# Dense attention of a hybrid encoder layer: value products three pairs behind the scores instead of two, and the dilated queries' gain multiplied on VectorE instead of GpSimd

## The chip, the cores and the metric

The kernel runs on one core of one Trainium2 chip. The metric is the device time of one execution in microseconds (us). The time before is the median of three runs, 1239.23 us (lowest 1236.90, highest 1239.25).

Short names of the engines, as the profile has them: PE is TensorE (matmul), PEld its weight loads, DVE is VectorE, ACT is ScalarE, POOL is GpSimd, SP is the engine that issues most DMAs.

## What is computed

One encoder layer on 1024 positions of 1024 features, all in float32. After a normalisation and one projection the heads go two ways. Group A (8 query heads, 2 key/value heads, 64 wide) is dense attention. Group B (8 heads) is a mixture of three dilated windows. Both outputs are normalised and projected, and a gated feed-forward block with a width-3 convolution follows. The parts that matter here:

```
hn = rms_norm(x, norm1_g);  proj = hn @ w_in          # -> qA kA vA qB kB vB
qa = apply_axial_rope(rms_norm(qa, qa_norm_g));  ka = the same with ka_norm_g
out_a = softmax(qa @ ka.T / 8) @ va                   # dense, all 1024 keys, per head
out_b = dilated_mixture_attention(rms_norm(qb, qb_norm_g), rms_norm(kb, kb_norm_g), vb)
x = x + concat(rms_norm(out_a), rms_norm(out_b)) @ w_out
x = x + conv_ffn(rms_norm(x, norm2_g))
```

The last step of the norm of qb, the multiplication by `qb_norm_g` (with the key's gain and the scale folded in), is what the second half of the change moves.

## The kernel before

The program runs in stages on one core: the input projection (0 to 212 us of the span), dense attention (212 to 387), dilated attention (387 to about 560), and then the output projection and the feed-forward block. All tensors of a stage lie at fixed offsets in two large arrays, `bigf` (float32) and `bigr` (float32 as TensorE multiplies it), and PSUM is one array `ps` of 8 banks of 512 columns. Float32 products are made of two or three products of a rounded high part and a rounded low part.

**Dense attention** is `a_main_bounded`, called for 16 groups g. A group is 128 queries (g // 2) of one key/value head (g % 2) with its four query heads, so a matmul has 512 columns. Its 1024 keys are taken in four pairs j of two tiles of 128 keys. For one pair:

- PE makes the scores: 4 matmuls (L763, L764) into two banks of PSUM. Two pairs of banks alternate, so the scores of pair n+2 wait until the exponential of pair n has read its banks.
- ACT takes the exponential of 1024 columns (L769) from PSUM into a float32 buffer `F_PB`.
- The high part is a copy of it (L773 on ACT; for j = 1 it is L771 on DVE) into `R_PHB`; the low part is a subtraction on DVE (L774) into `R_PLB`. There are two buffers `F_PB` and three of each of the others, used in turn.
- PE makes the value products `pv(j)`: 6 matmuls (L747), two for the high part of either tile and one for the low part. They accumulate over the group in one bank.

`pv(j)` is written two pairs behind the scores: `pv(0)` and `pv(1)` in steps 2 and 3 of their own group, `pv(2)`, `pv(3)` in steps 0 and 1 of the next. After `pv(3)` DVE copies the sums out (L757), PE turns them (L752), and DVE divides by the denominator (L792, L793). That turn (`o_turn`) is written into step 3 of the next group.

**Other work is spread over these groups.** The queries of the next group are split (L661 on ACT, L662 on DVE), turned on PE (L190) and copied (L678 on ACT). A table `spread`, by group and tile, holds what the projection left over: three additions (L444), the rotary step of two pieces of qa (POOL L528, L302; DVE L535, L538), two pieces of w_out (ACT L1060, DVE L1065), and the norm of the four pieces of qb: a square on ACT (L558), its mean on DVE (L510, L511), a root, `norm_at` on DVE (a 1-column copy L554, a 16-column copy L574, a multiplication of 1024 columns L575), and `gain` on POOL (L541, 1024 columns). The last two stand together in `spread[10 + i, 0]`. From group 14 on, the first head of the dilated stage is prepared: POOL splits its queries (L662 on POOL, after ACT's L661), PE turns them, POOL issues a DMA that copies keys (L868).

**What sets the order.** The instructions of an engine run in the order in which a scheduler in the framework puts them when the program is built; within an engine nothing overtakes. Code that is written later can so be put earlier. To hold a step back, the kernel writes one column of the step's destination from something that is ready late (`hold`, L1294; the copies L554, L1307, L1309). `now`, in `a_main_bounded`, is that something: the output of an earlier group, or the next group's queries.

The code for larger gains (`bounded` false) is in the program as well, behind a branch; it isn't run here.

Of the kernel before, what the change touches and what calls it, by code (L numbers as in the profile page):

```python
# [15 lines left out]
OP = mybir.AluOpType  # L16
# [28 lines left out]
R_XT = 0  # L45
# [37 lines left out]
R_VA = R_XT + 9248  # L83
R_PHB = (R_PH, R_PH + 1024, R_XT + 1024)
R_PLB = (R_PL, R_PL + 1024, R_XT + 3072)
F_PB = (O_F, O_F + 2560)
F_OT = O_F + 1024
# [47 lines left out]
def tile_encoder_layer(ctx, tc, x, w_in, gains, outg, norm1_g, norm2_g, w_out, w_up, conv_w, conv_b,  # L135
# [14 lines left out]
    def emit(bounded):  # L150
# [326 lines left out]
        def done(c, t0, u, late=None):  # L477
# [61 lines left out]

            def gain():  # L540
                gp.tensor_tensor(q3, q3, fp(O_GB, [0, 4], [0, 4], [1, 64]), op=OP.mult)  # L541

# [33 lines left out]

            return square_at, mean_at, root_at, refine_at, norm_at, gain

# [152 lines left out]

        pairs = [1]

        def a_main_bounded(g, prep, tail, late, plan, late_plan):
# [24 lines left out]
            for j in range(4):  # L759
# [6 lines left out]
                pairs[0] += 1  # L766
                p, ph, pl = F_PB[n % 2], R_PHB[n % 3], R_PLB[n % 3]
                slots[j] = ph, pl
# [6 lines left out]
                for kt in (2 * j, 2 * j + 1):  # L775
                    take(prep, plan[kt])
                    take(late, late_plan[kt])
                    now = f(qab((g - 1) // 2) + 256 * ((g - 1) % 2), 1) if 0 < kt < 7 else \
                        rf(R_Q2A + 512 * ((g + (kt == 7)) % 2), 1)
                    for step in spread.pop((g, kt), []):  # L780
                        step(now)
                step = tail.pop(0) if tail else None
                if step:
                    step()
                if j > 1:
                    pv(j - 2)

            return [lambda: pv(2), last, None, o_turn]

# [501 lines left out]
        if bounded:  # L1291
# [4 lines left out]
            def run(ts, o=None):  # L1296
                def at(now):
                    if o is not None:
                        hold(o, now)
                    for t in ts:  # L1300
# [6 lines left out]
                      (2, 2): [lambda now: vec.tensor_copy(f(F_KN[0], 1), now)] + run(first[:5]),  # L1307
                      (3, 0): run(first[5:6], F_KN[0]), (3, 3): run(first[6:], F_OS),
                      (3, 6): [lambda now: vec.tensor_copy(f(F_KN[0], 1), now)] + run(turns[:5]),  # L1309
                      (4, 5): run(turns[5:6], F_KN[0]), (5, 0): run(turns[6:], F_OS)}  # L1310
        for i, d in enumerate(deferred[2:]):
            square_at, mean_at, root_at, refine_at, norm_at, gain = done(*d, i)
            spread[5 + i, 2] = [square_at]
            spread[5 + i, 7] = [mean_at]
            if i == 3:
                spread[9, 3] = [root_at]
                spread[9, 7] = [refine_at]
            spread[10 + i, 0] = [norm_at, lambda now, gain=gain: gain()]

# [553 lines left out]
```

## Time and profile before

| | us |
|---|---|
| median of three runs | 1239.23 |
| the profiled execution's own time | 1239.64 |
| its span, first to last instruction | 1237.7 |
| outside the span | 1.9 |
| dense attention, 212 to 387 us: length | 175.0 |
| PE busy in it | 167.1 |
| DVE busy in it | 144.9 |
| ACT busy in it | 140.5 |
| POOL busy in it | 34.2 |

The profile is one execution, taken by the hardware profiler. Busy time of PE is the time covered by at least one matmul. Matmuls overlap: one of 512 columns is listed with about 0.39 us, and the next starts 0.23 us after it. So a waiting PE shows as idle a little later than it really had nothing to start, and slower matmuls show as a busy PE. The table of the stage by windows also has the granted clock of TensorE (PEclk, 1.00 is full).

In rows of the timeline the columns are start, duration, engine, line, operation, tiles and shapes, the number of instructions merged, and in brackets the idle time before with what ended it.

### The profile page before, as it was taken

To read this page: it belongs to the slowest core of one execution; us is meant where nothing else is said; L and a number is where in the kernel's file an instruction comes from. 1 tells how busy PE (TensorE), PEld (TensorE's weight loads), DVE (VectorE), ACT (ScalarE), POOL (GpSimd) and SP (SyncE) were. 2 spreads that over 40 slices of the span, in tenths; PEclk is the share of its full clock that TensorE was granted. 3 is DMA by queue.
4 is the path that set the end of the run, shared out by engine and by line. 5 is a ranking of instruction groups with operands and counts; after the bars stand their busy time and mean duration, and the time that the engine had idled before them with its cause. 6 is when DMAs were issued, how large, how long until landed. Compare 5 with 4: busy or idle time off the path is not lost.

```text
span 1237.7 us, 17828 instructions
## 1 busy us (share of the span) xinstructions
PE 1198.8 (97%) x6615; PEld 1010.7 (82%) x6615; DVE 1008.1 (81%) x1315; ACT 670.8 (54%) x968; POOL 403.6 (33%) x302
## 2 busy tenths in 40 slices
PE   7999999999899989999999999999999999999998
PEld 7999998666568988888788888888888888888886
DVE  4988687789888989656999999999999997876663
ACT  7856555789788766634554434453444544443341
POOL 1610114120223330011356666576755743000000
PEclk9999999999999999999999999999999999999999
DMA  7036403010004544422222332223232247977872
GB/s 277 25 101 159 112 4 75 1 33 17 1 9 108 134 112 133 156 81 77 94 90 89 111 106 106 88 98 114 94 110 94 88 160 253 353 235 245 280 234 92
DMA packets 120925, 147.00 MB, mean 119 GB/s; under 512 B 51009, under 2 KB 79489, under 8 KB 120321
## 3 DMA queue, kind: packets, MB, share of 16 engines
q1 hardware_dynamic: 119329, 140.05, 35.4%
q0 software_dynamic: 1504, 5.77, 2.3%
q8 instruction: 53, 0.87, 0.3%
q14 instruction: 39, 0.32, 0.1%
HBM read 107.25 MB, written 33.82 MB: 114 GB/s over the span
## 4 chain that ended last, share of the span: by engine, by line
PE 56%; DVE 17%; issue 5%; ACT 3%; DMA 1%; POOL 1%; SPq 0%; DVEq 0%; ACTq 0%; POOLq 0%
DVE bigf L1570 7%; PE ps L1537 6%; PE ps L1539 6%; PE ps L1538 6%; PE ps L1670 6%; PE ps L1669 6%; PE ps L1671 6%; PE ps L747 5%; DVE bigf L1541 2%; PE ps L1111 2%; PE ps L1112 2%; PE ps L1110 2%; DVE bigr L1521 2%; DVE bigr L774 2%; PE ps L763 2%
## 5 line engine op out<-in xcount | busy, mean ns | idle before, releaser
L1537 PE MATMUL ps<-bigr 128*128 128x512 f32 x616 | 241.1, 392 | 6.3 <-DVE bigf L1541 5.7
L1539 PE MATMUL ps<-bigr 128*128 128x512 f32 x616 | 239.7, 389 | 0.0
L1538 PE MATMUL ps<-bigr 128*128 128x512 f32 x616 | 239.7, 389 | 0.0
L1570 DVE SCALAR_TENSOR_TENSOR bigf<-bigf 128x768 f32<-128x768 f32 (+1 forms) x176 | 178.6, 1073 | 26.4 <-ACT bigf L1568 26.3
L1520 ACT ACTIVATE bigr<-bigf 128x512 fp32r<-128x512 f32 x154 | 93.2, 625 | 139.6 <-POOL bigf L1512 70.2
L1649 ACT ACTIVATE bigr<-bigf 128x1024 fp32r<-128x1024 f32 (+1 forms) x99 | 83.6, 867 | 116.0 <-PE ps L1671 74.2
L1537 PEld LDWEIGHTS ps<-bigr 128*128 128x128 f32 x616 | 115.6, 188 | 34.9 <-DVE bigf L1541 9.1
L1539 PEld LDWEIGHTS ps<-bigr 128*128 128x128 f32 x616 | 115.6, 188 | 24.2
L1538 PEld LDWEIGHTS ps<-bigr 128*128 128x128 f32 x616 | 115.7, 188 | 23.6
L432 PE MATMUL ps<-bigr 128*128 128x256 f32 x448 | 128.1, 286 | 1.1 <-ACT bigf L308 1.1
L433 PE MATMUL ps<-bigr 128*128 128x256 f32 x448 | 127.6, 285 | 0.4 <-DVE bigr L416 0.4
L1521 DVE TENSOR_TENSOR bigr<-bigf,bigr 128x512 fp32r<-128x512 f32 x112 | 125.1, 1134 | 3.2 <-ACT bigr L1520 2.8
L434 PE MATMUL ps<-bigr 128*128 128x256 f32 x448 | 127.4, 284 | 0.0
L1670 PE MATMUL ps<-bigr 128*128 128x512 f32 x308 | 119.8, 389 | 0.0
L1669 PE MATMUL ps<-bigr 128*128 128x512 f32 x308 | 119.8, 389 | 0.0
L1671 PE MATMUL ps<-bigr 128*128 128x512 f32 x308 | 119.8, 389 | 0.0
L1650 DVE TENSOR_TENSOR bigr<-bigf,bigr 128x1024 fp32r<-128x1024 f32 (+1 forms) x99 | 96.7, 995 | 26.4 <-ACT bigr L1649 24.3
L747 PE MATMUL ps<-bigr 128*66 128x512 f32 x384 | 103.6, 404 | 5.0 <-DVE bigr L774 4.8
L774 DVE TENSOR_TENSOR bigr<-bigf,bigr 128x1024 fp32r<-128x1024 f32 x64 | 84.6, 1333 | 16.1 <-ACT bigr L773 15.5
L432 PEld LDWEIGHTS ps<-bigr 128*128 128x128 f32 x448 | 86.5, 193 | 1.8 <-ACT bigf L308 1.5
L433 PEld LDWEIGHTS ps<-bigr 128*128 128x128 f32 x448 | 86.6, 193 | 0.6 <-DVE bigr L416 0.6
L434 PEld LDWEIGHTS ps<-bigr 128*128 128x128 f32 x448 | 86.6, 193 | 0.0
(230 smaller groups left out, 2513.2 us busy)
## 6 DMA issues: line engine op xcount, KB each, us to landing
bigf<-w_down SPq DMA_DIRECT2D x99, 256.0 KB, 4.3
bigf<-w_up SPq DMA_DIRECT2D x44, 512.0 KB, 3.6
bigf<-gscr SPq DMA_DIRECT2D x77, 256.0 KB, 4.2
gscr<-bigf SPq DMA_DIRECT2D x31, 512.0 KB, 2.6
bigf<-w_in SPq DMA_DIRECT2D x8, 1024.0 KB, 5.5
bigf<-x SPq DMA_DIRECT2D x15, 512.0 KB, 7.1
bigf<-w_out SPq DMA_DIRECT2D x8, 512.0 KB, 3.5
bigr<-bigr POOLq DMA_DIRECT2D x8, 512.0 KB, 4.4
```

Source lines behind the costliest of these rows:

```text
L432: mm(o, ah, wh, start=(k == 0 and t % 2 == 0 and n != 2), stop=False, skip_group_check=True)
L433: mm(o, ah, wl, start=False, stop=False, skip_group_check=True)
L434: mm(o, al, wh, start=False, stop=(k == 3), skip_group_check=True)
L747: mm(bank(ob)[0:66], r(w, 66), r(p + 512 * u, 512), start=(kt == 0 and i == 0), stop=(kt == 7 and i == 2))
L1521: (gp if n in (2, 4) and m > 3 else vec).tensor_tensor(rp(o + 512, [128, 4], [1, 128]), src, rfp(o, [128, 4], [1, 128]), op=OP.subtract)
L1537: mm(bank(b), wh, th, start=(k == 0 and n in (1, 5, 6, 7)), stop=False, skip_group_check=True)
L1538: mm(bank(b), wh, tl, start=False, stop=False, skip_group_check=True)
L1539: mm(bank(b), wl, th, start=False, stop=(k == 3), skip_group_check=True)
L1570: vec.scalar_tensor_tensor(f(a + o, n), f(i + d, n), w_, f(a + o, n), op0=OP.mult, op1=OP.add)
L1669: mm(o, ah, r(d, 512), start=(q == 0 and n in (1, 5, 2)), stop=False, skip_group_check=True)
L1670: mm(o, ah, r(d + 1024, 512), start=False, stop=False, skip_group_check=True)
L1671: mm(o, al, r(d, 512), start=False, stop=(q == NQ - 1), skip_group_check=True)
```

## The change

Two things.

1. `pv(j)` is written three pairs behind the scores. Only `pv(0)` is in its own group; `pv(1)`, `pv(2)`, `pv(3)` are in steps 0, 1, 2 of the next. `R_PHB` and `R_PLB` get a fourth buffer, chosen by j, and `F_PB` a third. `o_turn` of a group moves to step 0 of the group after the next (for the last group it stays in step 3 of what follows). `now` is the output of group g-2 instead of g-1, and the next group's queries throughout group 1. Some of the held steps get other places: the last two steps of the rotary of the first piece from (3, 0) and (3, 3) to (3, 2) and (3, 4), and of the second from (4, 5) and (5, 0) to (4, 4) and (4, 6).
2. `gain`, four multiplications of 1024 columns on POOL, becomes `gain_at` on DVE, one group later than its `norm_at`, with a 1-column copy and a 1-column hold ahead of each.

```
-R_PHB = (R_PH, R_PH + 1024, R_XT + 1024)
-R_PLB = (R_PL, R_PL + 1024, R_XT + 3072)
-F_PB = (O_F, O_F + 2560)
+R_PHB = (R_PH, R_PH + 1024, R_XT + 1024, R_XT + 13824)
+R_PLB = (R_PL, R_PL + 1024, R_XT + 3072, R_XT + 14848)
+F_PB = (O_F, O_F + 2560, O_F + 3584)
...
-            def gain():
-                gp.tensor_tensor(q3, q3, fp(O_GB, [0, 4], [0, 4], [1, 64]), op=OP.mult)
+            def gain_at(now):
+                tick(so, now)
+                vec.scalar_tensor_tensor(f(o, 1), f(so, 1), 0.0, f(o, 1), op0=OP.mult, op1=OP.add)
+                vec.tensor_tensor(q3, q3, fp(O_GB, [0, 4], [0, 4], [1, 64]), op=OP.mult)
...
-                p, ph, pl = F_PB[n % 2], R_PHB[n % 3], R_PLB[n % 3]
+                p, ph, pl = F_PB[n % 3], R_PHB[j], R_PLB[j]
...
-                    now = f(qab((g - 1) // 2) + 256 * ((g - 1) % 2), 1) if 0 < kt < 7 else \
+                    now = f(qab((g - 2) // 2) + 256 * (g % 2), 1) if 0 < kt < 7 and g > 1 else \
                         rf(R_Q2A + 512 * ((g + (kt == 7)) % 2), 1)
...
-                if j > 1:
-                    pv(j - 2)
-
-            return [lambda: pv(2), last, None, o_turn]
+                if j > 2:
+                    pv(j - 3)
+
+            behind, turn[:] = turn[:], [o_turn]
+            return [lambda: [t() for t in [lambda: pv(1)] + behind], lambda: pv(2), last, o_turn if g == 15 else None]
...
-                      (3, 0): run(first[5:6], F_KN[0]), (3, 3): run(first[6:], F_OS),
+                      (3, 2): run(first[5:6], F_KN[0]), (3, 4): run(first[6:], F_OS),
...
-                      (4, 5): run(turns[5:6], F_KN[0]), (5, 0): run(turns[6:], F_OS)}
+                      (4, 4): run(turns[5:6], F_KN[0]), (4, 6): run(turns[6:], F_OS)}
...
-            spread[10 + i, 0] = [norm_at, lambda now, gain=gain: gain()]
+            spread[10 + i, 0] = [norm_at]
+            spread[11 + i, 2] = [gain_at]
```

The order that the scheduler makes of it differs on every engine from the end of the projection to the first steps of the dilated stage; from there to the end it is the same. Lines of the changed kernel are up to four higher: scores L765 and L766, value products L749, high part L773 and L775, low part L776, copy out L759, turn L754, splits L663 and L664, norm L576 and L577, gain L542 and L543, holds L1297.

**PE, around the last pairs of group 1 and the first of group 2.** Before, the value products of two pairs often stand together, behind the scores of two pairs:

```order
L763 MATMUL ps<-bigr 128x512
L747 MATMUL ps<-bigr 66x512 x2
L764 MATMUL ps<-bigr 128x512
L190 MATMUL ps<-bigr 128x128 x2
L747 MATMUL ps<-bigr 66x512 x10
L763 MATMUL ps<-bigr 128x512
```

Now they stand pair by pair, six after every four scores:

```order
L749 MATMUL ps<-bigr 66x512 x6
L765 MATMUL ps<-bigr 128x512
L766 MATMUL ps<-bigr 128x512
L765 MATMUL ps<-bigr 128x512
L766 MATMUL ps<-bigr 128x512
L749 MATMUL ps<-bigr 66x512 x6
```

A row of ten holds the low part of one pair and the whole of the next; in the new order every row of six belongs to the pair whose scores were made three pairs before.

**DVE, at the multiplications of qb in groups 10 and 11.** Before, only the norm (L554, L574, L575) is on DVE, and POOL has the four rows L541 in a row of its own:

```order
L757 COPY bigf<-ps 66x512
L774 TENSOR_TENSOR bigr<-bigf,bigr 128x1024
L554 COPY bigf<-bigr 128x1
L574 COPY bigf<-bigf 128x16
L575 TENSOR_TENSOR bigf<-bigf 128x4x256
L774 TENSOR_TENSOR bigr<-bigf,bigr 128x1024
```

Now the gain of the piece before (hold L542, multiplication L543) stands between the subtractions L776, ahead of the next norm:

```order
L776 TENSOR_TENSOR bigr<-bigf,bigr 128x1024
L542 SCALAR_TENSOR_TENSOR bigf<-bigf 128x1
L556 COPY bigf<-bigr 128x1
L543 TENSOR_TENSOR bigf<-bigf 128x4x256
L776 TENSOR_TENSOR bigr<-bigf,bigr 128x1024
L759 COPY bigf<-ps 66x512
L576 COPY bigf<-bigf 128x16
L577 TENSOR_TENSOR bigf<-bigf 128x4x256
```

DVE gets two long instructions where it had one, and POOL's row of L541 is gone.

**PE, in group 14, where the first dilated head's queries and keys are turned (L190).** Before, all eight turns stand together behind the scores of the group's last pair, ahead of the value products:

```order
L764 MATMUL ps<-bigr 128x512
L190 MATMUL ps<-bigr 128x128 x8
L747 MATMUL ps<-bigr 66x512 x4
L752 MATMUL ps<-bigf 128x66 x4
L747 MATMUL ps<-bigr 66x512 x2
```

Now the second four, which wait for POOL's split of the queries, stand three value products later:

```order
L766 MATMUL ps<-bigr 128x512
L190 MATMUL ps<-bigr 128x128 x4
L749 MATMUL ps<-bigr 66x512 x3
L190 MATMUL ps<-bigr 128x128 x4
L749 MATMUL ps<-bigr 66x512 x3
```

On ACT, the high part that this split starts from (L661, now L663) stood ahead of the exponential of group 14's third pair and stands behind that exponential and its copy now.

More of the change, by code (lines that the diff above doesn't have):

```diff
@@ L575, in norm_at @@
                 vec.tensor_tensor(q3, q3, fp(fac, [4, 4], [1, 4], [0, 64]), op=OP.mult)
-            return square_at, mean_at, root_at, refine_at, norm_at, gain
+            return square_at, mean_at, root_at, refine_at, norm_at, gain_at
         dma(f(O_IDF, 128), ident)
@@ L730, in a_main @@
             return [lambda: pv(6), lambda: pv(7), lambda: o_norm(ob, 66, qab(b) + 256 * kv, ([64, 4], [1, 64]))]
-        pairs = [1]
+        pairs, turn = [1], []
         def a_main_bounded(g, prep, tail, late, plan, late_plan):
@@ L1307, in emit @@
                       (2, 2): [lambda now: vec.tensor_copy(f(F_KN[0], 1), now)] + run(first[:5]),
-                      (3, 0): run(first[5:6], F_KN[0]), (3, 3): run(first[6:], F_OS),
+                      (3, 2): run(first[5:6], F_KN[0]), (3, 4): run(first[6:], F_OS),
                       (3, 6): [lambda now: vec.tensor_copy(f(F_KN[0], 1), now)] + run(turns[:5]),
-                      (4, 5): run(turns[5:6], F_KN[0]), (5, 0): run(turns[6:], F_OS)}
+                      (4, 4): run(turns[5:6], F_KN[0]), (4, 6): run(turns[6:], F_OS)}
         for i, d in enumerate(deferred[2:]):
-            square_at, mean_at, root_at, refine_at, norm_at, gain = done(*d, i)
+            square_at, mean_at, root_at, refine_at, norm_at, gain_at = done(*d, i)
             spread[5 + i, 2] = [square_at]
```

## The prediction

> **What bounds the kernel now.** I read the page first, then the dense stage (the only one whose order changes) cut into windows, then PE's waits there, then the timeline at each wait.
>
> ```profile
> PE 1198.8 (97%) x6615; PEld 1010.7 (82%) x6615; DVE 1008.1 (81%) x1315; ACT 670.8 (54%) x968; POOL 403.6 (33%) x302
> ```
>
> PE is busy for 97% of the span, so only PE's waits and slow stretches can be won, and work moved between DVE, ACT and POOL counts only where PE waits for it. The windows say where that is; the columns are busy us of each engine in 20 us, then the granted clock, the DMAs' share and GB/s.
>
> ```profile
> core 0: us, PE busy (x) PEld busy (x) DVE busy (x) ACT busy (x) POOL busy (x), PEclk, DMA share, GB/s
> 212.00:232.00 20.00, 18.26 (x82) 12.63 (x81) 13.20 (x15) 12.80 (x16) 6.06 (x8) 0.91 0.00 0
> 252.00:272.00 20.00, 18.49 (x89) 12.58 (x88) 15.64 (x24) 15.37 (x19) 3.65 (x7) 1.00 0.12 27
> 272.00:292.00 20.00, 20.00 (x99) 13.99 (x98) 18.72 (x31) 18.52 (x22) 0.00 (x0) 1.00 0.08 26
> 292.00:312.00 20.00, 20.00 (x104) 14.01 (x102) 18.47 (x31) 18.59 (x23) 0.00 (x0) 1.00 0.00 1
> 312.00:332.00 20.00, 16.13 (x67) 10.11 (x67) 17.58 (x26) 12.96 (x17) 5.60 (x2) 0.91 0.00 1
> 352.00:372.00 20.00, 19.36 (x103) 13.39 (x101) 15.06 (x18) 16.45 (x22) 4.28 (x2) 1.00 0.06 14
> 212.00:387.00 175.00, 167.10 (x812) 115.24 (x811) 144.90 (x197) 140.52 (x169) 34.23 (x28) 0.98 0.07 18
> ```
>
> PE is idle for 175.0 - 167.1 = 7.9 us. The view of waits, for PE in the same stretch (total, times, longest):
>
> ```profile
> PE ps L747 <- DVE bigr L774: 4.8, 3, 2.5
> PE ps L763 <- ACT bigf L769: 2.3, 2, 1.7
> PE ps L190 <- DVE bigr L662: 0.6, 1, 0.6
> ```
>
> Six waits, 7.7 us: three of value products for the subtraction L774, two of scores for the exponential, one of a turn. The windows that lose have idle time of DVE and ACT in them as well; it is the order in which they serve, not their sum, that PE waits for. From 272 to 312 PE never stops, though DVE and ACT are at 18.5 us or more of 20.
>
> The timeline shows two of the waits and what follows them.
>
> ```profile
> 217.15 0.46 PE L190 MATMUL ps<-bigr 128*128 128x128 f32 x4
> 219.31 0.50 PE L763 MATMUL ps<-bigr 128*128 128x512 f32 x1 [1.71 <-ACT bigf L769]
> 219.65 3.65 PE L747 MATMUL ps<-bigr 128*66 128x512 f32 x10
> 225.73 2.48 PE L747 MATMUL ps<-bigr 128*66 128x512 f32 x10
> 315.57 4.52 DVE L774 TENSOR_TENSOR bigr<-bigf,bigr 128x1024 fp32r<-128x1024 f32 x2
> 315.79 3.22 POOL L541 TENSOR_TENSOR bigf<-bigf 128x1024 f32<-128x1024 f32 x1 [54.98 <-DVE bigf L575]
> 320.15 3.83 PE L747 MATMUL ps<-bigr 128*66 128x512 f32 x10 [2.49 <-DVE bigr L774]
> 321.79 2.54 DVE L771 CAST bigr<-bigf 128x1024 fp32r<-128x1024 f32 x1 [0.56 <-PE ps L747]
> ```
>
> The longest wait starts on POOL. While its gain multiplication ran (315.79 for 3.22 us), two subtractions took 4.52 us. Undisturbed, a pair takes 2.36:
>
> ```profile
> 324.43 2.36 DVE L774 TENSOR_TENSOR bigr<-bigf,bigr 128x1024 fp32r<-128x1024 f32 x2
> L575 DVE TENSOR_TENSOR bigf<-bigf 128x1024 f32<-128x1024 f32 x4 | 4.9, 1222 | 0.1
> L541 POOL TENSOR_TENSOR bigf<-bigf 128x1024 f32<-128x1024 f32 x4 | 12.1, 3026 | 81.3 <-DVE bigf L575 66.3 <-issue 15.0
> ```
>
> PE waited 2.49 us for that. After its two longest waits (1.71 and 2.49) ten value products took 3.65 and 3.83 us instead of 2.48, and only those windows have a clock of 0.91.
>
> **The change part by part.** *What goes.* With value products three pairs behind, the subtraction of a pair is wanted one pair later: four scores and six value products more. A value product starts 2.48 - 0.39 over 9, 0.232 us, after the one before (0.39 is one matmul's duration), so that is 10 x 0.232 = 2.3 us of slack. The waits for L774 were at most 2.49, and that one loses its 2.16 us of stretching (4.52 - 2.36) as well. The longer wait for the exponential came from its float32 buffer: with two buffers it waits for a subtraction two pairs back, with three for one three pairs back. The wait of the turn stood behind a subtraction that POOL stretched (352.59, below). For the shorter wait for the exponential, 0.6 us, no row shows such a cause; it lies within the allowance below.
>
> So I let all six go. Their price: 7.9 us of idle; in each of six waits the last matmul, which shows as busy for 0.39 us though the next could start after 0.232, hides 0.16 us, together 1.0; and the slow matmuls behind the long waits, 3.65 - 2.48 = 1.17 and 3.83 - 2.48 = 1.35, with about 0.4 more in the four scores that follow the first ten, 2.9. Sum 11.8 us.
>
> I count the slow stretches because they begin right at the end of the two longest waits and nowhere else in the stage. The Trainium skill, "TensorE: Matmul & The Clock Gate", Part 1 (The HAM clock gate), has the clock fall to half after an idle window of about 3.4 us. By that rule waits of 1.7 and 2.5 us need not slow anything, and the sum would lose the 2.9; the trace has slow matmuls behind both.
>
> *The gain on DVE.* It costs no PE time by itself. Per piece DVE gets a multiplication like L575 (1.22 us), a 1-column copy and a 1-column hold:
>
> ```profile
> L554 DVE COPY bigf<-bigr 128x1 f32<-128x1 f32 x9 | 1.2, 147 | 0.3
> L1294 DVE SCALAR_TENSOR_TENSOR bigf<-bigf 128x1 f32<-128x1 f32 x3 | 0.7, 239 | 2.2 <-POOL bigf L528 1.5 <-POOL bigf L302 0.6
> 352.59 2.69 DVE L774 TENSOR_TENSOR bigr<-bigf,bigr 128x1024 fp32r<-128x1024 f32 x1 [0.65 <-ACT bigr L773]
> 340.25 4.00 DVE L774 TENSOR_TENSOR bigr<-bigf,bigr 128x1024 fp32r<-128x1024 f32 x2
> 355.60 0.69 DVE L771 CAST bigr<-bigf 128x1024 fp32r<-128x1024 f32 x1
> ```
>
> 1.22 + 0.15 + 0.24 = 1.6, four times 6.4 us. It loses the stretching by POOL's four L541: 2.16, 2.54 - 0.69 = 1.85 at the copy L771 (0.69 at 355.60), 4.00 - 2.36 = 1.64 and 2.69 - 1.22 = 1.47, together 7.1. So DVE's sum hardly moves (-0.7 of 144.9). What hides the 1.6 in a group is DVE's free time: 175.0 - 144.9 = 30 us over 16 groups, 1.9 each, and three pairs of lag for the unevenness. Without that cover each gain would cost PE up to 1.6 us, and a slow stretch of 1.2 to 1.6 behind it.
>
> *The new wait on DVE.* The second rotary multiplication (L535) stood about three pairs behind the copy that starts POOL's part; it stands two pairs behind now.
>
> ```profile
> 246.26 1.30 POOL L528 TENSOR_TENSOR bigf<-bigf 128x512 f32<-128x512 f32 x1 [24.99 <-DVE bigf L1309]
> 247.64 6.14 POOL L302 TENSOR_TENSOR bigf<-bigf 128x128 f32<-128x128 f32 x8
> 253.82 1.22 DVE L535 TENSOR_TENSOR bigf<-bigf 128x1024 f32<-128x1024 f32 x1 [2.03 <-POOL bigf L302]
> ```
>
> POOL needs 253.78 - 246.26 = 7.5 us; two pairs on PE are 20 x 0.232 = 4.6, so DVE would wait about 2.9 in place of 2.03, in group 4. Queued behind it are the subtractions of pairs 1 and 2 of that group and the copy out of group 3; the value products of pair 1 want theirs three pairs (7 us) after its scores. That hides the wait; uncovered it would be 2.9 and a slow stretch, 4.3 at most. I take nothing.
>
> *Start of the stage.* The first scores of group 1 wait for the copied queries (L678), which in the new order stand behind the exponential of pair 2, no longer held by a subtraction:
>
> ```profile
> 215.35 1.05 ACT L773 ACTIVATE bigr<-bigf 128x1024 fp32r<-128x1024 f32 x1
> 216.30 0.59 ACT L678 ACTIVATE bigr<-ps 128x512 fp32r<-128x512 f32 x1
> 218.24 1.02 ACT L769 ACTIVATE bigf<-ps 128x1024 f32<-128x1024 f32 x1 [1.04 <-DVE bigr L774]
> ```
>
> ACT: 216.40 + 1.02 + 0.59 = 218.0; PE is through its turns at 217.15 + 0.46 = 217.6. A wait of 0.4 stays of the 1.71; I take 0.4, with 0 and 1.7 as ends.
>
> *Group 14.* The split of the dilated queries now starts on ACT behind an exponential and a copy, and PE turns them three value products and four turns after the scores:
>
> ```profile
> 366.07 1.03 ACT L769 ACTIVATE bigf<-ps 128x1024 f32<-128x1024 f32 x1 [0.60 <-PE ps L764]
> 367.13 1.06 ACT L773 ACTIVATE bigr<-bigf 128x1024 fp32r<-128x1024 f32 x1
> 364.84 0.63 ACT L661 ACTIVATE bigr<-bigf 128x512 fp32r<-128x512 f32 x1
> 365.60 2.08 POOL L662 TENSOR_TENSOR bigr<-bigf,bigr 128x512 fp32r<-128x512 f32 x1 [11.40 <-ACT bigr L661]
> 376.78 1.29 POOL L662 TENSOR_TENSOR bigr<-bigf,bigr 128x512 fp32r<-128x512 f32 x1 [1.13 <-ACT bigr L661]
> 368.17 0.80 PE L190 MATMUL ps<-bigr 128*128 128x128 f32 x8
> ```
>
> On the clock of these rows: copy done 368.2, L661 to 368.8, POOL to 370.2 or 371.0 (1.29 or 2.08 from 368.9). PE wants it at 368.17 + 0.3 + 3 x 0.232 = 369.2. The wait is 1.0 to 1.8; I take 1.4, and 0 as the other end if ACT gets there earlier.
>
> *ACT and the hand-over.* One piece of w_out (L1060, 1024 columns like L773's 1.06 us) ran on ACT ahead of the stage and is in group 6 now, and ACT was already at 18.5 of 20 there. The last turn of group 14 stands behind a subtraction and a longer dilated operation. I allow 1.0 for both, 0 to 3. New waits: 0.4 + 1.4 + 1.0 = 2.8.
>
> *The sum:* 1239.64 - 11.8 + 2.8 = **1230.6 us**. The profiled execution is 0.4 above the median, which I leave in, since a time is measured to about 0.2% (2.5 us): smaller differences count as none. The stages behind start earlier by what is won; their orders are the same and PE is their bound too.
>
> **The rivals.** *All cover holds* (nothing new waits): 1239.64 - 11.8 = 1227.8, at the least about 1227. For it: the waits are single and DVE and ACT have 30 us free. Against: group 14's row arithmetic. Chance 0.15.
>
> *The slow stretches aren't the waits' doing and stay:* the clock falls by a count of its own, and as many matmuls run slow somewhere in the stage: 1230.6 + 2.9 = 1233.5. Against: where they begin. Chance 0.08. This is how it would go by the page named above.
>
> *ACT becomes the bound of groups 5 to 9.* Between 272 and 312 DVE and ACT are at 93%. The added L1060, about 1.1, and a PE that no longer pauses ahead of that stretch, would make PE wait one to two us in each of two or three groups: about 4 us, 1234.6. For it: the two windows. Against: PE lost nothing there before. Chance 0.14.
>
> *Nothing is won (within 0.2%):* the waits at group 4 (2.9 and 1.4 of slow matmuls) and group 14 (1.8 and 1.4) come in full, with 1.7 at the start: 4.3 + 3.2 + 1.7 = 9.2 in place of the 1.8 taken, so 1230.6 + 7.4 = 1238.0. Chance 0.07.
>
> *Slower.* The gains push DVE over PE in groups 11 to 14. DVE's mean share of a group is 144.9 / 16 = 9.1 us, 0.4 of it POOL's stretching; less that, with a gain, 10.3. PE's is (16 + 24) x 0.232 and about 0.6 of turns, 9.9. If DVE enters group 11 behind by more than the 2.3 us of lag, PE waits for the gain in each of four groups, 1.6 and a slow stretch of 1.4 each: 12.0, so 1242.6. Against: 4 x 0.4 us of excess is under 2.3. Chance 0.05.
>
> **How the numbers follow.** The forecast, 1229 to 1233, has 0.51; the others as above. Faster by over 0.2%: 0.51 + 0.15 + 0.08 + 0.14 = 0.88; same 0.07; slower 0.05. The range 1227 to 1237 leaves out the slower case, most of "nothing won" and the outer ends of the two next to it.
>
> **What would show it right or wrong.** In the profile after: PE's waits for L774's successor (L776) gone from its list, the clock 1.00 in all windows of the stage, no subtraction over 1.5 us from 310 to 355, DVE's wait for POOL in group 4 without one of PE behind it, and a wait of L190 for POOL of 1 to 2 us in group 14. Wrong would be: waits of PE for ACT in groups 5 to 9, slow matmuls without a long wait ahead of them, or a wait for L776 in groups 11 to 14.

## The result and the profile after

The changed kernel takes 1229.22 us (median of 5 runs, 1227.34 to 1231.12), the kernel before 1238.38 (median of 5, 1236.90 to 1239.25). The ratio is 0.9931, 95% interval 0.9917 to 0.9944: faster by 9.2 us by the medians and by 8.5 us by the ratio, which is not formed from the two medians. The forecast was 1230.6, 9.0 us under the profiled execution before. The profiled execution took 1229.49 us with a span of 1227.6, against 1239.64 and 1237.7.

The page's first line, then the windows of the dense stage (busy us of each engine, then the granted clock):

```profile
PE 1193.6 (97%) x6615; PEld 1008.0 (82%) x6615; DVE 1005.8 (82%) x1327; ACT 671.2 (55%) x968; POOL 393.6 (32%) x298
```

```profile
212.00:232.00 20.00, 19.72 (x93) 13.71 (x92) 18.15 (x24) 18.30 (x21) 0.00 (x0) 1.00 0.00 0
252.00:272.00 20.00, 18.08 (x89) 12.09 (x88) 16.66 (x22) 15.18 (x19) 5.81 (x8) 1.00 0.17 41
312.00:332.00 20.00, 20.00 (x99) 13.90 (x98) 19.32 (x28) 18.22 (x23) 0.00 (x0) 1.00 0.00 1
352.00:372.00 20.00, 18.71 (x102) 13.21 (x100) 14.59 (x16) 17.17 (x23) 6.02 (x4) 1.00 0.28 65
212.00:377.00 165.00, 161.51 (x806) 112.79 (x805) 144.97 (x212) 142.66 (x172) 26.21 (x26) 1.00 0.09 23
```

The clock is 1.00 throughout. The first window and the one from 312, which had lost 1.7 and 3.9 us of PE, lose 0.3 and nothing; the one from 252 loses 1.9 instead of 1.5 and the one from 352 1.3 instead of 0.6. PE's idle time in the stage is 165.0 - 161.5 = 3.5 us instead of 7.9. The view of waits of PE in the stage:

```profile
PE ps L754 <- DVE bigf L759: 1.9, 2, 1.4
PE ps L190 <- POOL bigr L664: 1.3, 1, 1.3
PE ps L1001 <- DVE bigf L759: 0.4, 1, 0.4
PE ps L765 <- ACT bigr L680: 0.3, 1, 0.3
```

No value product (L749) waits any more. PE waits for turns: of a group's output (L754), of the dilated queries (L190), of the next queries (L765 by way of the copy L680); L1001 lies in the dilated stage. The largest of them was not in the forecast. DVE, then PE, in group 4:

```profile
254.90 1.23 DVE L535 TENSOR_TENSOR bigf<-bigf 128x1024 f32<-128x1024 f32 x1 [2.45 <-POOL bigf L302]
256.04 1.22 DVE L776 TENSOR_TENSOR bigr<-bigf,bigr 128x1024 fp32r<-128x1024 f32 x1
257.18 1.22 DVE L538 TENSOR_TENSOR bigf<-bigf 128x1024 f32<-128x1024 f32 x1
258.31 1.22 DVE L776 TENSOR_TENSOR bigr<-bigf,bigr 128x1024 fp32r<-128x1024 f32 x1
259.45 0.68 DVE L759 COPY bigf<-ps 66x512 f32<-66x512 f32 x1
...
260.18 0.46 PE L754 MATMUL ps<-bigf 66*128 66x66 f32 x4 [1.45 <-DVE bigf L759]
270.70 0.46 PE L754 MATMUL ps<-bigf 66*128 66x66 f32 x4 [0.47 <-DVE bigf L759]
```

DVE stands 2.45 us for POOL. The two subtractions behind it are late, but their value products come three pairs after the scores and are not. The copy out of group 3 stands behind both, and its turn has no such lag: PE waits 1.45 us. Before, PE waited 1.51 us behind the same multiplication, for a subtraction; the wait has changed its name and stands about half a group later.

**Where the time went.** From the start of the first scores to that of the last value product the stage takes 166.6 us (210.97 to 377.56) instead of 173.7 (212.39 to 386.06): 7.1 us won. At the hand-over 0.7 more: the second dilated head's value products start 13.3 us after the last dense one, not 14.0. The two belong together: in the new order twelve small matmuls of the dilated stage (four turns, eight scores) stand inside the stretch that they used to follow. The other 2.3 us of this pair of profiles, 1.4 ahead of the stage and 0.9 within the dilated stage, lie where the order is the same; the profiles of the experiments differ by as much in these places.

### The profile page after: what moved, and what is told of

The parts are those of the page before. It is cut to its first block, busy times and chain, and to the rows that moved or that the text cites. A ratio compares the mean times of both kernels' runs of the same rounds, so it can differ in the third digit from the quotient of the medians.

```text
span 1227.6 us, 17810 instructions
## 1 busy us (share of the span) xinstructions
PE 1193.6 (97%) x6615; PEld 1008.0 (82%) x6615; DVE 1005.8 (82%) x1327; ACT 671.2 (55%) x968; POOL 393.6 (32%) x298
## 4 chain that ended last, share of the span: by engine, by line
PE 62%; DVE 19%; issue 7%; ACT 6%; DMA 3%; POOL 2%; SPq 0%; DVEq 0%; ACTq 0%; POOLq 0%
DVE bigf L1574 7%; PE ps L1541 7%; PE ps L1543 6%; PE ps L1542 6%; PE ps L1674 6%; PE ps L1675 6%; PE ps L1673 6%; PE ps L749 6%; DVE bigf L1545 2%; PE ps L1114 2%; PE ps L1115 2%; PE ps L1113 2%; DVE bigr L1525 2%; PE ps L765 2%; PE ps L766 2%
## 5 line engine op out<-in xcount | busy, mean ns | idle before, releaser
L749 PE MATMUL ps<-bigr 128*66 128x512 f32 x384 | 100.2, 394 | 0.0
L776 DVE TENSOR_TENSOR bigr<-bigf,bigr 128x1024 fp32r<-128x1024 f32 x64 | 79.6, 1248 | 7.6 <-ACT bigr L775 7.1
```

The source lines that it names most:

```text
L749: mm(bank(ob)[0:66], r(w, 66), r(p + 512 * u, 512), start=(kt == 0 and i == 0), stop=(kt == 7 and i == 2))
```

## The experiments

My theory: PE's waits went for two reasons. The lag and the third exponential buffer take the deadline from VectorE's subtractions, and the multiplication off GpSimd ends the stretching of VectorE; the slow matmuls followed the long waits and went with them. Rivals: one of the halves does it all; the third buffer does it; the slow stretches come by a count of their own. A second question is what the changed kernel still loses, 1.45 + 0.47 in groups 4 and 5 and 1.29 in group 14.

Executions differ by several us, so beside the time each row has the length of the stage in its profile, start of the first scores to start of the last value product. (Every kernel with the lag has the twelve small matmuls of the dilated stage in it, about 0.7 us; the three without the lag don't.) The ratio is to the kernel before on the same chip. The changed kernel was profiled twice; its stage took 166.59 and 166.57 us.

| kernel | median us | ratio, 95% interval | stage, us |
|---|---|---|---|
| before | 1238.4 | | 173.67 |
| third exponential buffer alone | 1236.9 | 0.9995 (0.9985 to 1.0005) | 172.10 |
| changed, two exponential buffers | 1234.3 | 0.9975 (0.9965 to 0.9986) | 171.77 |
| lag alone | 1232.3 | 0.9957 (0.9942 to 0.9972) | 169.09 |
| gain on VectorE alone | 1232.4 | 0.9954 (0.9938 to 0.9970) | 168.38 |
| changed | 1229.2 | 0.9931 (0.9917 to 0.9944) | 166.59 |
| changed, again | 1231.2 | 0.9940 (0.9922 to 0.9957) | 166.57 |
| changed, later second rotary | 1229.6 | 0.9944 (0.9928 to 0.9959) | 166.59 |
| changed, early table | 1229.6 | 0.9929 (0.9913 to 0.9945) | 165.79 |
| changed, earlier last gain | 1230.0 | 0.9940 (0.9926 to 0.9954) | 165.33 |
| later rotary and earlier gain | 1229.1 | 0.9931 (0.9917 to 0.9946) | 165.35 |
| early table and earlier gain | 1228.3 | 0.9920 (0.9903 to 0.9937) | 164.53 |
| all three | 1228.9 | 0.9920 (0.9907 to 0.9934) | 164.67 |
| changed, with three blocks | 1239.6 (one run) | | 174.30 |

### The two halves

The lag alone (the changed kernel with the multiplication back on GpSimd):

```
...
-            spread[10 + i, 0] = [norm_at]
-            spread[11 + i, 2] = [gain_at]
+            spread[10 + i, 0] = [norm_at, lambda now, gain=gain: gain()]
```

> The changed kernel with the queries' last multiplication back on GpSimd, right behind the norm as it was: only the lag of three pairs, its buffers and its order are left. My theory: most of the gain is the lag's. Of before's waits the one at the start of the stage (1.71 us and its slow matmuls), the one at the second rotary multiplication (1.51) and the small ones go, and the stretched subtractions (4.5 us for two instead of 2.36) come back, but three pairs of lag (2.3 us more slack) hide all or nearly all of the 2.49 that PE waited for them. So about the changed kernel's time, ratio to before 0.993 to 0.9955, and subtractions over 1.5 us between 305 and 350 us without a wait of PE over 0.5 us. Rival: the stretching by GpSimd is what PE waits for there, whatever the lag: then the waits of 2.49, 0.79 and 0.62 us and the slow matmuls stay, about 4 to 5 us of the 9, ratio 0.997.

Measured: 0.9957, just past the upper end of what I expected. PE's two largest waits, then DVE, POOL and PE where GpSimd multiplies (lines as in the kernel before):

```profile
PE ps L752 <- DVE bigf L757: 2.0, 2, 1.6
PE ps L190 <- DVE bigr L662: 1.8, 1, 1.8
```

```profile
321.74 3.23 POOL L541 TENSOR_TENSOR bigf<-bigf 128x1024 f32<-128x1024 f32 x1 [7.51 <-DVE bigf L575]
322.72 3.33 DVE L774 TENSOR_TENSOR bigr<-bigf,bigr 128x1024 fp32r<-128x1024 f32 x1
325.97 0.41 DVE L662 TENSOR_TENSOR bigr<-bigf,bigr 128x256 fp32r<-128x256 f32 x1
326.44 0.53 PE L190 MATMUL ps<-bigr 128*128 128x128 f32 x4 [1.77 <-DVE bigr L662]
328.50 0.63 PE L763 MATMUL ps<-bigr 128*128 128x512 f32 x1
328.92 0.63 PE L764 MATMUL ps<-bigr 128*128 128x512 f32 x1
```

The subtraction is stretched from 1.22 to 3.33 us, and no value product waits for it, as I said. But the split of the next queries stands behind it and its turn has no lag: 1.77 us, and matmuls 0.43 us apart instead of 0.23 behind that. That no wait over 0.5 us would come there was wrong. So the lag hides a late subtraction from the value products only.

The gain alone (the kernel before with the multiplication on VectorE):

```
...
-            spread[10 + i, 0] = [norm_at, lambda now, gain=gain: gain()]
+            spread[10 + i, 0] = [norm_at]
+            spread[11 + i, 2] = [gain_at]
```

> The kernel before, with only the queries' last multiplication moved to VectorE (in group 11 to 14, as in the changed kernel); value products follow by two pairs, with the old buffers and rotary places. My theory: the longest wait (2.49 us) and its slow matmuls go with GpSimd's multiplications, but with two pairs of lag the 1.6 us that each adds to VectorE shows in part, and the waits at the start (1.71) and at the second rotary multiplication (1.51) stay: 2 to 4 us of the 9 are won, ratio 0.9965 to 0.9985. Rival: the move alone brings the gain, ratio 0.994 or less. Other rival: with two pairs of lag VectorE's extra load costs what GpSimd's stretching did, ratio 0.999 to 1.001.

Measured: 0.9954, more than my theory gave. The waits of PE:

```profile
PE ps L765 <- ACT bigf L771: 2.3, 2, 1.7
PE ps L749 <- DVE bigr L776: 1.9, 2, 1.5
```

The waits of 2.49, 0.79 and 0.62 us in groups 10 to 13 became one of 0.36 us. The added 1.6 us per piece is covered by two pairs of lag but for that 0.36 us; the waits at the start and in group 4 stayed at 1.71 and 1.54. The halves win 4.6 and 5.3 us of the stage alone and 7.1 together; with the twelve small matmuls set aside, the lag wins 5.3 and both together 7.8. So they overlap. Both remove the waits of 0.79 and 0.62 us; the lag alone leaves 1.77 us and slow matmuls in place of the longest wait, so at these places most of what it wins the gain wins too. And the wait of 1.29 us in group 14 stands in no profile of one half, only where both are in.

### The third buffer

```
-F_PB = (O_F, O_F + 2560)
+F_PB = (O_F, O_F + 2560, O_F + 3584)
...
-                p, ph, pl = F_PB[n % 2], R_PHB[n % 3], R_PLB[n % 3]
+                p, ph, pl = F_PB[n % 3], R_PHB[n % 3], R_PLB[n % 3]
```

> The kernel before with a third buffer for the exponentials, and nothing else of the change. My theory: the wait for the exponential at the start of the stage (1.71 us, and 1.2 to 1.4 us of slow matmuls behind it) goes or falls under 0.5 us, since the exponential of a pair then waits for a subtraction three pairs back; the waits for subtractions stay. 1.5 to 3 us won, ratio 0.9975 to 0.9988. Rival: the wait only changes its name (the value products then wait for the same subtraction at the same place), ratio 0.9995 to 1.0005.

Measured: 0.9995; as a whole my theory fell, though the stage in its profile is 1.6 us shorter. The wait at the start did go (0.26 and 0.55 us in place of 1.71), but the scheduler's order moved with the buffer, and in group 4 the copy out now waited behind the rotary step:

```profile
246.93 1.23 DVE L535 TENSOR_TENSOR bigf<-bigf 128x1024 f32<-128x1024 f32 x1 [2.95 <-POOL bigf L302]
249.41 0.46 PE L752 MATMUL ps<-bigf 66*128 66x66 f32 x4 [2.81 <-DVE bigf L757]
```

Slow matmuls followed from 251.29 us on.

The other way round, the changed kernel with two exponential buffers (`F_PB[n % 2]`):

> The changed kernel with two buffers for the exponentials instead of three. My theory: an exponential again waits for the subtraction two pairs back, so where VectorE is late the scores stop whatever the lag of the value products: the wait at the start of the stage comes back (about 1.7 us and its slow matmuls), and one at the second rotary multiplication in group 4; 3 to 5 us of the 9 are lost, ratio 0.9955 to 0.9975. Rival: the buffer does not matter, the lag does: ratio 0.993 as the changed kernel.

Measured: 0.9975, at the upper end of what I expected, and 5.2 us of the stage lost. PE's three longest waits:

```profile
PE ps L765 <- ACT bigr L680: 1.8, 1, 1.8
PE ps L190 <- POOL bigr L664: 1.3, 1, 1.3
PE ps L765 <- ACT bigf L771: 1.0, 1, 1.0
```

ACT's exponentials waited 8.0 us for subtractions, in eight places:

```profile
ACT bigf L771 <- DVE bigr L776: 8.0, 8, 2.1
```

PE waited 1.01 us for one of them, and 1.79 for the copied queries in group 5. So lag and buffer belong together: without the third buffer the exponential takes over the deadline that the value product lost.

### What is left in groups 4 and 5

The second rotary step later, so that the copy out goes ahead of the addition:

```
-                      (4, 4): run(turns[5:6], F_KN[0]), (4, 6): run(turns[6:], F_OS)}
+                      (4, 6): run(turns[5:6], F_KN[0]), (5, 0): run(turns[6:], F_OS)}
```

> The changed kernel with the second rotary piece's multiplication and addition put back two steps (from steps 4 and 6 of group 4 to step 6 of group 4 and step 0 of group 5), so that the copy out of group 3 (L759) stands ahead of the addition and of one subtraction on VectorE; nothing else moves. My theory: what is left of PE's idle time in group 4 is the turn of group 3's output behind that copy; the copy then ends about 2 us earlier, and PE's wait of 1.45 us there goes (the one of 0.47 a group later may stay). The time falls by 1.6 to 2.2 us under the changed kernel's: ratio to before 0.9913 to 0.992. Rival: VectorE's wait for GpSimd (2.45 us) costs the same wherever the copy stands, since a value product or an exponential then waits for a subtraction: PE's wait stays over 1 us under another name, ratio 0.993.

Measured: the stage took 166.59 us, as without the edit; the rival was right. The wait of 1.45 us went, and this one came (ACT, then PE):

```profile
265.64 1.06 ACT L560 ACTIVATE bigf<-bigf 128x1024 f32<-128x1024 f32 x1 [2.45 <-DVE bigf L556]
267.50 0.59 ACT L680 ACTIVATE bigr<-ps 128x512 fp32r<-128x512 f32 x1
268.15 0.50 PE L765 MATMUL ps<-bigr 128*128 128x512 f32 x1 [1.23 <-ACT bigr L680]
```

DVE is as late as it was; its one-column copy that releases ACT's square is late, ACT's copy of the queries stands behind the square, and PE waits for that.

So the root, DVE's wait for POOL: the table is made four steps earlier.

```
-                      (3, 2): run(first[5:6], F_KN[0]), (3, 4): run(first[6:], F_OS),
-                      (3, 6): [lambda now: vec.tensor_copy(f(F_KN[0], 1), now)] + run(turns[:5]),
+                      (3, 2): run(first[5:6], F_KN[0]) + [lambda now: vec.tensor_copy(f(F_KN[0], 1), now)] + run(turns[:1]),
+                      (3, 4): run(first[6:], F_OS) + run(turns[1:5]),
```

> The changed kernel with the second rotary piece's table made as soon as the first piece's multiplication has read the old one (in step 2 of group 3 instead of step 6), and its turned products right behind the first piece's addition (step 4): GpSimd starts about 3 us earlier, and nothing else moves but one 1-column copy on VectorE and one fill on GpSimd. My theory: the root of PE's two waits in groups 4 and 5 (1.45 and 0.47 us) is the 2.45 us in which VectorE waits for GpSimd at the second rotary multiplication, after which VectorE is busy without a gap for 18 us; started earlier, GpSimd is done in time, VectorE's wait falls under 0.3 us, and both waits of PE go. First score to last value product: 166.6 - 2.0 = 164.6 us (1.92 and 0.16 for each wait). Rival: VectorE has too much to do there even without the wait, so one of PE's waits stays or moves on as in the run with the later multiplication: 166 us or more. The whole time, about 1227.5 by the theory, is known less well, since executions differ by 2 us ahead of and behind this stage.

Measured: the stage fell by 0.8 us, less than half of what I expected. POOL and DVE in groups 3 and 4:

```profile
244.57 2.15 POOL L528 TENSOR_TENSOR bigf<-bigf 128x512 f32<-128x512 f32 x1 [3.29 <-DVE bigf L1311]
246.84 8.29 POOL L302 TENSOR_TENSOR bigf<-bigf 128x128 f32<-128x128 f32 x8
...
245.48 3.73 DVE L776 TENSOR_TENSOR bigr<-bigf,bigr 128x1024 fp32r<-128x1024 f32 x2
255.16 1.23 DVE L535 TENSOR_TENSOR bigf<-bigf 128x1024 f32<-128x1024 f32 x1 [0.78 <-POOL bigf L302]
```

and POOL in the changed kernel:

```profile
247.53 2.48 POOL L528 TENSOR_TENSOR bigf<-bigf 128x512 f32<-128x512 f32 x1 [6.15 <-DVE bigf L1312]
250.09 4.78 POOL L302 TENSOR_TENSOR bigf<-bigf 128x128 f32<-128x128 f32 x8
```

Counted from the first scores (212.00 here, 210.97 there) POOL starts 4.0 us earlier, but ends only 0.8 earlier: its eight products take 8.29 us instead of 4.78, while DVE now works beside them nearly to their end, where it stood waiting for half of the time, and DVE's two subtractions take 3.73 us instead of 2.35. DVE's wait falls from 2.45 to 0.78 us, PE's from 1.45 to 0.56; the one of 0.47 a group later is 0.41.

### What is left in group 14

The last gain half a group earlier:

```
-            spread[11 + i, 2] = [gain_at]
+            spread[(13, 6) if i == 3 else (11 + i, 2)] = [gain_at]
```

> The changed kernel with the last of the four query multiplications half a group earlier (step 6 of group 13 instead of step 2 of group 14): the split of the first dilated head's queries needs it. The order of group 14 moves with it. My theory: PE's wait of 1.29 us in group 14 for GpSimd's part of the split is there because ScalarE's part stands behind that multiplication; it falls under 0.3 us, and 1.0 to 1.5 us are won: ratio to before 0.992 to 0.9925. Rival: the split is late because of ScalarE's exponentials ahead of it, or the two multiplications now both in group 13 make PE wait there: ratio 0.993 or more.

Measured: the stage fell by 1.26 us to 165.33, as expected; the time was 0.9940, in the rival's range, and shows nothing of it. In the changed kernel, then in this one:

```profile
353.98 1.22 DVE L543 TENSOR_TENSOR bigf<-bigf 128x1024 f32<-128x1024 f32 x1
355.70 0.61 ACT L663 ACTIVATE bigr<-bigf 128x512 fp32r<-128x512 f32 x1
356.39 1.78 POOL L664 TENSOR_TENSOR bigr<-bigf,bigr 128x512 fp32r<-128x512 f32 x1 [93.63 <-ACT bigr L663]
358.22 0.53 PE L190 MATMUL ps<-bigr 128*128 128x128 f32 x4 [1.29 <-POOL bigr L664]
```

```profile
349.09 1.23 DVE L543 TENSOR_TENSOR bigf<-bigf 128x1024 f32<-128x1024 f32 x1
354.00 0.63 ACT L663 ACTIVATE bigr<-bigf 128x512 fp32r<-128x512 f32 x1
354.71 2.06 POOL L664 TENSOR_TENSOR bigr<-bigf,bigr 128x512 fp32r<-128x512 f32 x1 [90.39 <-ACT bigr L663]
357.32 0.80 PE L190 MATMUL ps<-bigr 128*128 128x128 f32 x8
```

In the changed kernel ACT's part follows the gain and a copy of an exponential; with the gain out of the way the scheduler put it ahead of an exponential, and PE does not wait.

### Together

> Both of the two edits before in one kernel. My theory: the two waits are independent, so the gains add: 2.6 to 3.7 us under the changed kernel, about 1226, ratio to before 0.990 to 0.9913, and PE's idle time from the first scores to the last value product under 1 us. Rival: one of the two moves only passes the wait on: ratio 0.992.

The later rotary with the earlier gain: stage 165.35 us. The gain's 1.25 us are won, the rotary's edit again wins nothing: the rival. The early table with the earlier gain:

> The same with the last query multiplication half a group earlier as well. My theory: first score to last value product 163.3 us, with no wait of PE over 0.5 us in it but the one at its start (0.26). Of the 3.3 us won against the changed kernel some 1 to 1.5 are lost again in the dilated stage, where VectorE waited 1.5 and 1.8 us for a table from memory in the two runs with this edit: about 1227, ratio to before 0.990 to 0.992. Rival: those waits differ from one execution to the next whatever the order, and all of it is kept: 1225.5 to 1226.5, ratio 0.990 or less.

Measured: stage 164.53 us, so that the two gains add (0.80 + 1.26 = 2.06), though not to 163.3, since the early table won less. The time is 1228.32 us, against 1231.19 for the changed kernel on the same chip; this is the best version that the runs point to, but the intervals 0.9903 to 0.9937 and 0.9922 to 0.9957 overlap, so only the stage's length shows it ahead of the changed kernel. All three edits:

> The early table, the earlier last query multiplication and the later second rotary multiplication together: against the kernel with the first two, the copy out of group 3 goes ahead of the addition and one subtraction on VectorE, and nothing else moves. My theory: with VectorE waiting only 0.8 us for GpSimd, what stays of PE's wait for that copy (0.58 us) goes, and as VectorE is 1.7 us less late than in the run with the later multiplication alone, the wait for the copied queries that came up there (1.25 us) does not: first score to last value product 163.5 to 164.0 us, against 164.53. Rival: VectorE has no free time in groups 4 and 5 and the wait moves on: 164.5 us or more. The time about 1228, ratio 0.990 to 0.993.

Measured: 164.67 us, the rival: PE's wait of 0.58 us went, one of 0.48 for the copied queries came. What is left there is VectorE's own lateness: between these two orders only what waits for it changes.

### What differs from one execution to the next

> The changed kernel once more, for a second profile and more times beside the two above. Ratio 0.992 to 0.9945. My theory: the waits of PE in the dense stage are a matter of the order and come back within 0.1 us (0.3, 1.45, 0.47, 1.29), while the slow stretch ahead of the stage (0.9 to 1.6 us lost behind one and the same wait of 2.56 us) and VectorE's waits for tables in the dilated stage (0.4 to 3.3 us in the runs so far) differ from the first profile. Rival: those two are as fixed for one kernel as the waits are, and both come back within 0.2 us.

Measured: ratio 0.9940. The four waits came back as 0.28, 1.55, 0.47 and 1.29 us and the stage to 0.02 us. DVE's waits for tables were 1.3 us in all instead of 2.5. The slow stretch ahead of the stage came back within 0.2 us, as the rival had it: from the end of the wait of 2.57 us there to the first scores it is 13.74 us in the first profile and 13.65 in this one. Over the fourteen profiles that distance is 13.65 to 13.95 us, behind a wait of always 2.55 to 2.59; the spread of the first scores, 210.3 to 213.1 us, arises almost wholly ahead of that wait, which ended at 196.6 to 199.1. In the dilated stage the same instruction waits for the same table in some profiles and not in others (later rotary alone, then with the earlier gain):

```profile
444.44 1.21 DVE L982 TENSOR_TENSOR bigf<-ps,bigf 128x1024 f32<-128x1024 f32 x1
```

```profile
444.83 1.22 DVE L982 TENSOR_TENSOR bigf<-ps,bigf 128x1024 f32<-128x1024 f32 x1 [1.79 <-DMA bigf<-tee]
```

These waits are 0.4 to 3.3 us of DVE in a profile, and what follows goes with them: with the changed order the distance from the last dense value product to the first matmul of the feed-forward block is 202.9 us at 1.3 us of waiting, 204.1 at 2.5 and 205.5 to 205.6 at 3.3. They hide a gain of one us in a time. The two profiles with 3.3 us, both with the earlier gain, are also the only ones with a stretch of half clock in the dilated stage, from 449.55 and 447.52 us; behind the second of these waits PE had waited 1.59 and 1.60 us for the late VectorE. Whether the earlier gain makes the waits more likely (3.3 us in both of its first two profiles, 2.6 and 2.7 in the next two, 3.2 with the blocks below, 1.3 to 2.9 in the six others with the lag) is open.

### The slow matmuls

```
+        def block(n):
+            def at(now):
+                vec.tensor_copy(f(F_OS, 1), now)
+                vec.tensor_reduce(f(F_OS + 1000, n), fp(F_OS, [0, n], [1, 512]), axis=AX.X, op=OP.max)
+            return at
+        for g0, n in ((9, 6), (11, 9), (13, 12)):
+            spread.setdefault((g0, 5), []).append(block(n))
```

> The changed kernel with three long instructions added on VectorE, one each in groups 9, 11 and 13: reductions over 3072, 4608 and 6144 elements a partition (by the reduction over 1024 elements, 1.22 us, about 3.5, 5.3 and 7.0 us each), whose results are not used. Behind each, PE's value products wait for late subtractions; with about 3 us of slack the waits should be about 0.5, 2 and 4 us. My theory on the clock: so far every wait of PE in this stage of 1.71 us and more was followed within 2 us by ten-odd matmuls at half rate (1.3 to 1.55 us lost) and none of 1.56 us and less was; so a spell follows each single wait over 1.7 us here and none of a shorter wait, and a wait of 4 us is followed by the same 1.3 to 1.6 us, not by more. Rival: the spells come by a count of their own: then spells and waits do not fall together. Rival by the Trainium skill, page TensorE: Matmul & The Clock Gate, Part 1 (The HAM clock gate), with an idle window of about 3.4 us: only the longest wait is followed by slow matmuls.

The three instructions took 3.35, 4.95 and 6.55 us. PE did not wait behind the first, waited 1.11 us behind the second and 3.29 behind the third:

```profile
341.78 0.50 PE L765 MATMUL ps<-bigr 128*128 128x512 f32 x1 [1.11 <-ACT bigf L771]
362.43 0.75 PE L190 MATMUL ps<-bigr 128*128 128x128 f32 x4 [3.29 <-DVE bigr L664]
```

Only the third is followed by slow matmuls, and they cost 2.1 us or a little more, not the 1.3 to 1.6 that I expected. This kernel alone does not tell my rule from the rival's longer window, as no wait of 2 us came. The other profiles do. In the dense stage of all fourteen the waits of 1.71, 1.71, 1.77, 1.79, 2.49, 2.81 and 3.29 us were each followed within 2 us by slow matmuls that cost 1.3 to 1.6 us (2.1 or more after the longest); the fourteen waits of 1.2 to 1.56 us were followed by none, and no slow stretch stood without such a wait. Many of these are one and the same wait in several kernels. That the spells come by a count of their own, apart from the waits, is refuted for this stage.

But a count has a part in it. In the traces' own record of the granted clock every stretch of half clock in the middle of a kernel lasts 3.41 us (6.83 after the longest wait, two of 3.41 on end), and within a profile they start whole multiples of 3.41 us apart: 200.11, 220.59 and 319.58 us in the kernel before, 6 and 29 steps. So the clock is decided window by window, on a grid that the waits don't move. Here are, in the kernel before, the first slow stretch of the stage with the window ahead of it, and then the two slow windows with the blocks (the third column from the right is the clock):

```profile
217.18:220.59 3.41, 1.70 (x11) 1.11 (x10) 2.94 (x3) 2.37 (x4) 3.41 (x4) 1.00 0.00 0
220.59:224.01 3.42, 3.42 (x10) 2.13 (x9) 2.32 (x3) 2.32 (x4) 0.68 (x2) 0.50 0.00 0
```

```profile
361.29:364.70 3.41, 2.27 (x11) 1.64 (x12) 3.41 (x8) 0.60 (x1) 0.00 (x0) 0.50 0.00 0
364.70:368.12 3.42, 3.42 (x9) 2.24 (x10) 3.42 (x5) 2.62 (x4) 0.00 (x0) 0.50 0.00 0
```

What counts is PE's idle time within one such window, not the length of a wait. Over the fourteen profiles, from 20 to 1215 us, each of the 17 windows at full clock in which PE was idle for more than 1.75 us was followed by one at half clock, none of the 4843 with under 1.58 us was, and 7 of the 15 between were. A wait of 1.2 to 1.56 us by itself stays under that, wherever the window starts; a longer wait can be cut in two by a window's edge (the wait of 2.81 us had 1.74 in the window that counted). The grid also sets what a stretch costs: the wait ahead of the dense stage is the same in all profiles, and its 3.41 us of half clock began from 0.06 us before to 1.81 us after its end. The earlier they began, the less PE lost: from its end to the first scores it is 13.65 us at the earliest and 13.92 to 13.95 where they began 0.65 us or more after it.

## Why the prediction was right, and where it wasn't

The working gave 11.8 us of old waits and 2.8 of new ones, 9.0 won. Measured in the stage and the hand-over: 7.1 + 0.7 = 7.8.

**What goes: 11.8.** Right in size: no value product and no exponential is waited for. The slow matmuls counted at 2.9 us cost about 1.5 and 1.35 us in the profile of before and are gone. They were said to begin right at the end of the two waits; the first began 1.26 us after it, with the next window of the clock (220.59). The rival that they stay (1233.5) was wrong. Beside it stood the Trainium skill, "TensorE: Matmul & The Clock Gate", Part 1 (The HAM clock gate), by whose idle window of about 3.4 us waits of 1.7 us would slow nothing. The traces differ: all seven waits that were followed by slow matmuls were shorter, and 1.71 us, half of a window, was enough. That none follows what is left in group 4 has some luck in it: PE's idle time in one window there is 1.32 and 1.48 us in the two profiles of the changed kernel, and 1.59 was enough once elsewhere.

**The start: 0.4.** Measured 0.28 idle and 0.16 in the last matmul: right, for the reason given (L680).

**Group 14: 1.4.** Measured 1.29 + 0.16: right in size. The cause was given as the exponential and the copy ahead of ACT's part, and they do stand ahead of it; the earlier gain adds that the place of the last piece's gain, which the split needs, decides whether they do.

**DVE's wait for POOL: nothing taken.** This step failed, and with it the sign "without one of PE behind it". The wait was put at 2.9 us and came at 2.45; it was called covered because the value products want their subtractions three pairs later. True, but among what queues behind it the prediction itself named the copy out of group 3, and then gave only the subtractions a deadline. That copy is wanted by a turn that the lag does not move. It cost 1.45 + 0.47 us and 0.16 for each, 2.2.

**ACT and the hand-over: 1.0 allowed.** Not needed: from 272 to 352 us PE never stopped. The rival with ACT as the bound of groups 5 to 9 (1234.6) did not come.

So the new waits were 0.44 + 1.45 + 2.24 = 4.1 us, not 2.8, and 11.8 - 4.1 = 7.7 is what the stage and the hand-over show. That the median came out closer to the forecast is luck, the scatter ahead of and behind the stage: the second series, 1231.19 against 1238.74, gives 7.6.

**The gain on DVE.** DVE's busy time in the stage did not move (144.9 and 145.0; -0.7 was the estimate), and no subtraction between 305 and 356 us took over 1.23. The gain alone shows that the cover was larger than the rival of a DVE over PE (1242.6) supposed: even with two pairs of lag the 1.6 us a group left PE waiting only 0.36 us.

## What to carry to other kernels

A longer lag between producer and consumer relaxes only the instructions that feed that consumer. List everything that stands behind a late instruction on its engine, and give each its own deadline: here the value products had 2.3 us more, and the turns of outputs and queries, behind the same subtractions, had nothing. Where two edits remove the same waits, their gains don't add, and a buffer that one of them needs can show nothing when it is tried alone.

## What the runs showed of the hardware

- The granted clock of TensorE fell to half for whole windows of 3.41 us, on a grid that runs through the kernel. A window followed at half clock whenever PE had been idle for more than 1.75 us of the one before at full clock (17 of 17) and never after less than 1.58 us (4843 windows). In the dense stage that meant waits of 1.71 us or more and none of 1.56 or less; the slow matmuls, 0.43 us apart instead of 0.23, began up to 1.9 us after the wait, and one wait costs itself and 1.3 to 1.6 us more, or 2.1 and more when two windows are slow. The Trainium skill, "TensorE: Matmul & The Clock Gate", Part 1 (The HAM clock gate), calls the monitoring window free-running; the grid in these records agrees.
- VectorE's subtractions (two inputs) and GpSimd's multiplications slow each other: 1.22 us became 3.33 beside a GpSimd multiplication of 3.23, and eight GpSimd products took 8.29 us beside a busy VectorE and 4.78 beside one that waited. Starting GpSimd 4.0 us earlier brought its end only 0.8 us earlier.
- In the two profiles of the changed kernel the dense stage is the same to 0.02 us, while the stretches around it differ by up to 3 us over the fourteen profiles. An edit worth one us showed in the stage's length and not in the time.
